# A Huber loss streamed through one core: half-row tiles in bf16 with POOL subtracting, against whole-row tiles in f32 worked in pieces by DVE and ACT

## The chip, the core and the metric

The kernel runs on one core of a Trainium2 chip. The metric is the device time of one execution in microseconds, the median of several runs. A core has compute engines with instruction queues of their own: VectorE (DVE), ScalarE (ACT), GpSimd (POOL) and TensorE (PE, unused here); SyncE (SP) issues transfers. The core's 16 DMA engines move data between HBM and the on-chip memory of 128 partitions. A transfer is issued by an instruction in the queue of SP, ACT or POOL and then runs by itself; semaphores tell when it has landed.

## The reference

```python
def reference(pred, target):            # both 8192 x 8192, float32
    delta = 1.0
    diff = pred - target
    abs_diff = np.abs(diff)
    return np.where(abs_diff <= delta, 0.5 * diff**2, delta * (abs_diff - 0.5 * delta))
```

Every element is read from two inputs and one result is written: 536.87 MB in, 268.44 MB out. Both kernels use the identity that with c the difference clamped to [-1, 1] (or min(|d|, 1)), the loss is c²/2 + max(|d| - 1, 0).

## The kernel before, in words

The 8192 rows are cut into 64 row tiles of 128 rows, one row on each partition, 8192 columns. A row tile's inputs come as two halves of 4096 columns, each a transfer of 2 MB per input (`emit_loads`, L46 to L58): `a` always from SP's queue, `b` from SP's for the first half and from ACT's for the second. The pools of `a` and `b` have three half-row buffers each (L37, L38), so one and a half row tiles of input fit.

For each row tile the loop (L92 to L115) first issues the loads of the next tile, then finishes the tile before (`do_tail`, L65: on ACT the square at L68 and the Relu of |d| - 1 at L69, on DVE the sum at L70), then has POOL subtract the halves and write the difference as bf16 (L103), then ACT takes the absolute value (L108) and DVE the minimum with 1 (L109). The result `sfull` is bf16; `flush` (L60) has POOL's queue issue its store, a transfer that casts bf16 to f32 on the way out (L63). So three compute engines share a tile, all on whole rows of 8192 columns in bf16 except for POOL's half rows.

What sets the order: each engine works through its queue as written. A load waits for a buffer, which POOL's subtraction at L103 frees. The subtraction waits for its two halves. The store at L63 stands in POOL's queue between subtractions.

The last two tiles (L117 to L226) are written out by hand in pieces of 2048 and 1024 columns. Some pieces go the way described, others on DVE alone (a clamp, a fused multiply-add and a product, as at L197, L200 and L203), and each piece has its own store from POOL's queue (L179, L191).

Of the kernel before, what the change touches and what calls it, by code (L numbers as in the profile page):

```python
# [6 lines left out]


@with_exitstack
def kernel(  # L10
# [6 lines left out]
    nc = tc.nc  # L17
    P = 128
    fp32 = mybir.dt.float32
    bf16 = mybir.dt.bfloat16  # L20
    Alu = mybir.AluOpType
    Act = mybir.ActivationFunctionType

    n_rows, n_cols = pred.shape
    COLS = 4096
    n_ct = n_cols // COLS
    SQRT_HALF = 0.70710678118654752
# [4 lines left out]
    n_rt = pred_t.shape[0]  # L32

    neg1 = nc.alloc_sbuf_tensor("huber_neg1_bf16", [P, 1], bf16)
    nc.gpsimd.memset(neg1.ap(), -1.0)
# [6 lines left out]
    loads = {}  # L42
    pending_tail = []
    pending_store = []

    def emit_loads(i):  # L46
        if i >= n_rt:
            return
        tl = []
        for j in range(n_ct):  # L50
            c0 = j * COLS
            a = pool_a.tile([P, COLS], fp32)
            b = pool_b.tile([P, COLS], fp32)
            nc.sync.dma_start(out=a, in_=pred_t[i, :, c0 : c0 + COLS])
            beng = nc.sync if j == 0 else nc.scalar
            beng.dma_start(out=b, in_=targ_t[i, :, c0 : c0 + COLS])
            tl.append((a, b))
        loads[i] = tl  # L58

    def flush(limit):  # L60
        while len(pending_store) > limit:
            r, pi = pending_store.pop(0)
            nc.gpsimd.dma_start(out=out_t[pi, :, :], in_=r)  # L63

    def do_tail(limit):  # L65
        while len(pending_tail) > limit:
            s, d, pi = pending_tail.pop(0)
            nc.scalar.activation(out=s, in_=s, func=Act.Square, scale=SQRT_HALF)  # L68
            nc.scalar.activation(out=d, in_=d, func=Act.Relu, bias=neg1.ap())  # L69
            nc.vector.tensor_tensor(out=s, in0=s, in1=d, op=Alu.add)  # L70
            pending_store.append((s, pi))

    def act_path(d, s):
        nc.scalar.activation(out=d, in_=d, func=Act.Abs)
        nc.vector.tensor_scalar(
            out=s, in0=d, scalar1=1.0, scalar2=None, op0=Alu.min
        )
        nc.scalar.activation(out=s, in_=s, func=Act.Square, scale=SQRT_HALF)
        nc.scalar.activation(out=d, in_=d, func=Act.Relu, bias=neg1.ap())
        nc.vector.tensor_tensor(out=s, in0=s, in1=d, op=Alu.add)  # L80

    def dve_path(d, s):
        nc.vector.tensor_scalar(
            out=s, in0=d, scalar1=-1.0, scalar2=1.0, op0=Alu.max, op1=Alu.min
        )
        nc.vector.scalar_tensor_tensor(
            out=d, in0=s, scalar=-0.5, in1=d, op0=Alu.mult, op1=Alu.add
        )
        nc.vector.tensor_tensor(out=s, in0=s, in1=d, op=Alu.mult)

    emit_loads(0)
    for i in range(n_rt - 2):  # L92
        dfull = pool_d.tile([P, n_cols], bf16)
        sfull = pool_s.tile([P, n_cols], bf16)

        emit_loads(i + 1)

        do_tail(0)

        for j in range(n_ct):  # L100
            c0 = j * COLS
            a, b = loads[i][j]
            nc.gpsimd.tensor_tensor(  # L103
                out=dfull[:, c0 : c0 + COLS], in0=a, in1=b, op=Alu.subtract
            )
        del loads[i]

        nc.scalar.activation(out=dfull, in_=dfull, func=Act.Abs)  # L108
        nc.vector.tensor_scalar(  # L109
            out=sfull, in0=dfull, scalar1=1.0, scalar2=None, op0=Alu.min,  # L110
        )

        flush(1)

        pending_tail.append((sfull, dfull, i))  # L115

    i62 = n_rt - 2  # L117
    i63 = n_rt - 1
    H = n_cols // 2

    d62 = pool_d.tile([P, n_cols], bf16, tag="dfull")
    s62 = pool_s.tile([P, n_cols], bf16, tag="sfull")

    emit_loads(i63)
    do_tail(0)

    for j in range(n_ct):
        c0 = j * COLS
        a, b = loads[i62][j]
        nc.gpsimd.tensor_tensor(  # L130
            out=d62[:, c0 : c0 + COLS], in0=a, in1=b, op=Alu.subtract
        )
    del loads[i62]

    flush(1)

    Q = 2048
    dq = [d62[:, k * Q : (k + 1) * Q] for k in range(4)]
    sq = [s62[:, k * Q : (k + 1) * Q] for k in range(4)]
    nc.scalar.activation(out=dq[0], in_=dq[0], func=Act.Abs)  # L140
    nc.vector.tensor_scalar(out=sq[0], in0=dq[0], scalar1=1.0, scalar2=None, op0=Alu.min)  # L141
    nc.vector.tensor_scalar(  # L142
        out=sq[1], in0=dq[1], scalar1=-1.0, scalar2=1.0, op0=Alu.max, op1=Alu.min
    )
# [45 lines left out]
    def st(lo, hi, s):  # L190
        nc.gpsimd.dma_start(out=out_t[i63, :, lo:hi], in_=s)  # L191
# [65 lines left out]
```

## Time and profile before

| | |
|---|---|
| median of the runs | 1923.07 us (4 runs, 1922.99 to 1923.16) |
| profiled execution | 1923.1 us, its span 1921.3 us |
| busy: DVE, ACT, POOL | 851.0, 1326.3, 1288.9 us |
| bytes moved by the DMA engines | 805.42 MB, mean 419 GB/s over the span |
| loads from SP's queue (q1) | 402.67 MB |
| loads from ACT's queue (q10) | 134.22 MB |
| stores from POOL's queue (q0) | 268.44 MB written |

The profile is of one execution. The span runs from its first to its last recorded instruction or transfer; the run's own time has 1.8 us more. A row of windows has the two ends of a stretch and its length, then for DVE, ACT and POOL the busy time and the number of instructions, the granted clock of TensorE, the mean busy share of the 16 DMA engines (packets that overlap can take it above 1) and the GB/s that they moved. Packets count with their ends, so windows of a few microseconds scatter. A row of groups has line, engine, operation, output and input, shapes and count, then the busy time in us and the mean of one in ns, then the idle time before and what ended it. In the timeline the columns are start, duration (over all merged instructions, waits between them included), engine, line and operation; SPq and ACTq are the queues' transfer-issuing instructions. In the list of DMA queues the columns after the name are packets, MB and the time that the packets took as a share of 16 engines' span.

### The profile page before, as it was taken

How to read it: one execution, taken by the hardware profiler on the slowest of the kernel's cores; microseconds unless marked ns; L12 is line 12 of the kernel's file. 1: busy time of each engine (PE TensorE's matmuls, PEld its weight loads, DVE VectorE, ACT ScalarE, POOL GpSimd, SP SyncE). 2: the span in 40 equal slices, each digit the busy share in tenths (PEclk: the TensorE clock that was granted, in tenths of full speed). 3: DMA queues.
4: the chain of work that ended last, by engine and by line, in shares of the span. 5: the costliest groups of instructions: out<-in, count | busy, mean ns of one | idle time of the engine just before them, and what ended most of it. 6: DMA issues, size and time to landing. Idle time of an engine off the chain costs nothing.

```text
span 1921.3 us, 1430 instructions
## 1 busy us (share of the span) xinstructions
DVE 851.0 (44%) x146; ACT 1326.3 (69%) x202; POOL 1288.9 (67%) x207
## 2 busy tenths in 40 slices
DVE  0344354453443534534435345344353443444566
ACT  2866767668677676686776866767768667676674
POOL 5686676766866767667677676676766866767664
DMA  9999999999999999999999999999999999999996
GB/s 405 377 422 423 423 427 423 426 424 425 425 423 426 426 424 426 420 426 425 426 422 427 425 425 425 424 424 425 427 424 425 424 423 425 425 425 424 425 429 271
DMA packets 47100, 805.42 MB, mean 419 GB/s; under 512 B 5233, under 2 KB 5233, under 8 KB 5489
## 3 DMA queue, kind: packets, MB, share of 16 engines
q1 hardware_dynamic: 27648, 402.67, 53.9%
q0 software_dynamic: 10224, 268.44, 32.9%
q10 hardware_dynamic: 9216, 134.22, 16.3%
q14 instruction: 12, 0.09, 0.0%
HBM read 536.87 MB, written 268.44 MB: 419 GB/s over the span
## 4 chain that ended last, share of the span: by engine, by line
ACT 51%; DVE 29%; issue 18%; DMA 1%; POOL 1%; ACTq 0%; POOLq 0%; SPq 0%
DVE sfull L109 28%; ACT dfull L108 23%; ACT sfull L68 22%; ACT dfull L69 5%; DMA b<-in_target_dram 1%; POOL dfull L103 1%; DVE s L153 1%; DVE s L142 0%; DVE sfull L70 0%; DVE s L194 0%; DVE d L147 0%; DVE d L159 0%; ACT d L158 0%; ACT s L195 0%; ACTq L252 0%
## 5 line engine op out<-in xcount | busy, mean ns | idle before, releaser
L103 POOL TENSOR_TENSOR dfull<-a,b 128x4096 bf16<-128x4096 f32 x124 | 1213.7, 9803 | 588.1 <-issue 559.0
L68 ACT ACTIVATE sfull<-sfull 128x8192 bf16<-128x8192 bf16 x62 | 435.9, 7030 | 532.8 <-DVE sfull L109 532.8
L70 DVE TENSOR_TENSOR sfull<-sfull,dfull 128x8192 bf16<-128x8192 bf16 x62 | 274.4, 4426 | 860.6 <-ACT dfull L69 860.6
L109 DVE TENSOR_SCALAR sfull<-dfull 128x8192 bf16<-128x8192 bf16 x62 | 528.7, 8527 | 194.8 <-ACT dfull L108 194.8
L108 ACT ACTIVATE dfull<-dfull 128x8192 bf16<-128x8192 bf16 x62 | 434.8, 7012 | 33.0 <-POOL dfull L103 33.0
L69 ACT ACTIVATE dfull<-dfull,huber_neg_bf 128x8192 bf16<-128x8192 bf16 x62 | 440.6, 7106 | 0.0
L63 POOL DMA_DIRECT2D out_dram<-sfull x62 | 35.7, 575 | 3.8 <-DVE sfull L70 3.8
L130 POOL TENSOR_TENSOR d<-a,b 128x4096 bf16<-128x4096 f32 x2 | 19.6, 9838 | 9.5 <-issue 9.5
L175 POOL TENSOR_TENSOR d<-a,b 128x2048 bf16<-128x2048 f32 (+1 forms) x5 | 18.1, 3643 | 0.1
L191 POOL DMA_DIRECT2D out_dram<-s x5 | 2.7, 540 | 11.7 <-DVE s L217 5.9
L153 DVE TENSOR_SCALAR s<-d 128x2048 bf16<-128x2048 bf16 x1 | 9.8, 9842 | 0.0
L142 DVE TENSOR_SCALAR s<-d 128x2048 bf16<-128x2048 bf16 x1 | 9.3, 9320 | 0.0
L179 POOL DMA_DIRECT2D out_dram<-s x4 | 2.2, 551 | 10.5 <-DVE s L152 4.2
L195 ACT ACTIVATE s<-s 128x2048 bf16<-128x2048 bf16 x1 | 1.9, 1911 | 8.1 <-DVE s L194 8.1
L162 DVE TENSOR_TENSOR s<-s,d 128x2048 bf16<-128x2048 bf16 x1 | 6.1, 6053 | 2.7 <-ACT d L158 2.7
L157 ACT ACTIVATE s<-s 128x2048 bf16<-128x2048 bf16 x1 | 1.9, 1910 | 6.0 <-DVE s L153 6.0
L145 ACT ACTIVATE s<-s 128x2048 bf16<-128x2048 bf16 x1 | 1.9, 1910 | 4.1 <-DVE s L141 4.1
L194 DVE TENSOR_SCALAR s<-d 128x2048 bf16<-128x2048 bf16 x1 | 3.3, 3276 | 0.0
L147 DVE SCALAR_TENSOR_TENSOR d<-s,d 128x2048 bf16<-128x2048 bf16 x1 | 2.3, 2293 | 0.0
L159 DVE SCALAR_TENSOR_TENSOR d<-s,d 128x2048 bf16<-128x2048 bf16 x1 | 2.3, 2283 | 0.0
L200 DVE SCALAR_TENSOR_TENSOR d<-s,d 128x2048 bf16<-128x2048 bf16 x1 | 2.3, 2278 | 0.0
L108 ACT ACT_TABLE_LOAD x1 | 1.3, 1283 | 1.2 <-PEq L241 1.2
(32 smaller groups left out, 34.7 us busy)
## 6 DMA issues: line engine op xcount, KB each, us to landing
a<-in_pred_dram SPq DMA_DIRECT2D x128, 2048.0 KB, 18.0
out_dram<-sfull POOLq DMA_DIRECT2D x62, 4096.0 KB, 20.1
b<-in_target_dram ACTq DMA_DIRECT2D x64, 2048.0 KB, 13.8
b<-in_target_dram SPq DMA_DIRECT2D x64, 2048.0 KB, 25.2
out_dram<-s POOLq DMA_DIRECT2D x7, 1024.0 KB, 4.9
out_dram<-s POOLq DMA_DIRECT2D x2, 512.0 KB, 5.0
```

What stands on the lines that cost most here:

```text
L63: nc.gpsimd.dma_start(out=out_t[pi, :, :], in_=r)
L68: nc.scalar.activation(out=s, in_=s, func=Act.Square, scale=SQRT_HALF)
L69: nc.scalar.activation(out=d, in_=d, func=Act.Relu, bias=neg1.ap())
L70: nc.vector.tensor_tensor(out=s, in0=s, in1=d, op=Alu.add)
L103: nc.gpsimd.tensor_tensor(out=dfull[:, c0 : c0 + COLS], in0=a, in1=b, op=Alu.subtract)
L108: nc.scalar.activation(out=dfull, in_=dfull, func=Act.Abs)
L109: nc.vector.tensor_scalar(out=sfull, in0=dfull, scalar1=1.0, scalar2=None, op0=Alu.min,)
L130: nc.gpsimd.tensor_tensor(out=d62[:, c0 : c0 + COLS], in0=a, in1=b, op=Alu.subtract)
L142: nc.vector.tensor_scalar(out=sq[1], in0=dq[1], scalar1=-1.0, scalar2=1.0, op0=Alu.max, op1=Alu.min)
L153: nc.vector.tensor_scalar(out=sq[2], in0=dq[2], scalar1=1.0, scalar2=None, op0=Alu.min)
L162: nc.vector.tensor_tensor(out=sq[2], in0=sq[2], in1=dq[2], op=Alu.add)
L175: nc.gpsimd.tensor_tensor(out=d63[:, lo:hi], in0=a[:, o0:o1], in1=b[:, o0:o1], op=Alu.subtract)
```

## The change

The kernel is written anew. It computes the same formula, in f32 throughout:

- A tile is a whole row tile, `a` and `b` in f32 of 8192 columns, three of each (`DEPTH`). A load is one transfer of 4 MB, all loads in SP's queue, `b` ahead of `a`. The loads of the last tile are split in four.
- Compute goes by pieces of 2048 columns, in place. `first` has DVE subtract (L58 of the new file) and clamp to [-1, 1] (L59), and ACT take Abs, Relu with bias -1 and the square (L62 to L64). `second` has DVE form 0.5 c² + max(|d| - 1, 0) (L69). `second` of a piece is written two pieces after its `first`, so it stands behind the first steps of the two following pieces in DVE's queue, of the next tile where need be.
- The stores copy f32 and are issued from ACT's queue, two of half a row for each tile (L53); the last tile has five.
- The loads of tile j + 3 are written after tile j's last `second`. `b` of it waits for that; `a` for the two stores of tile j.
- POOL is left with nothing in the loop. The order of SP, DVE and ACT is that of the code.

```diff
+P = 128
+ROW = 8192
+PIECE = 2048
+DEPTH = 3
...
-    pool_a = ctx.enter_context(tc.tile_pool(name="sbuf_a", bufs=3))
-    pool_b = ctx.enter_context(tc.tile_pool(name="sbuf_b", bufs=3))
-    pool_d = ctx.enter_context(tc.tile_pool(name="sbuf_d", bufs=2))
-    pool_s = ctx.enter_context(tc.tile_pool(name="sbuf_s", bufs=3))
+    pool_a = ctx.enter_context(tc.tile_pool(name="pool_a", bufs=DEPTH))
+    pool_b = ctx.enter_context(tc.tile_pool(name="pool_b", bufs=DEPTH))
...
+    def load(i, halves):
+        A[i] = pool_a.tile([P, ROW], f32, name="a")
+        B[i] = pool_b.tile([P, ROW], f32, name="b")
+        for lo, hi in halves:
+            nc.sync.dma_start(out=B[i][:, lo:hi], in_=targ_t[i, :, lo:hi])
+            nc.sync.dma_start(out=A[i][:, lo:hi], in_=pred_t[i, :, lo:hi])
...
-            nc.gpsimd.dma_start(out=out_t[pi, :, :], in_=r)
+    def store(i, lo, hi):
+        nc.scalar.dma_start(out=out_t[i, :, lo:hi], in_=A[i][:, lo:hi])
+
+    def first(i, lo, hi):
+        a, b = A[i][:, lo:hi], B[i][:, lo:hi]
+        nc.vector.tensor_tensor(out=a, in0=a, in1=b, op=Alu.subtract)
...
-            nc.gpsimd.tensor_tensor(
-                out=dfull[:, c0 : c0 + COLS], in0=a, in1=b, op=Alu.subtract
-            )
...
+            out=b, in0=a, scalar1=-1.0, scalar2=1.0, op0=Alu.max, op1=Alu.min
         )
+        nc.scalar.activation(out=a, in_=a, func=Act.Abs)
+        nc.scalar.activation(out=a, in_=a, func=Act.Relu, bias=neg1)
+        nc.scalar.activation(out=b, in_=b, func=Act.Square)
+    def second(i, lo, hi):
+        a, b = A[i][:, lo:hi], B[i][:, lo:hi]
         nc.vector.scalar_tensor_tensor(
+            out=a, in0=b, scalar=0.5, in1=a, op0=Alu.mult, op1=Alu.add
         )
...
+    with tc.manual_schedule(engines={Eng.SP, Eng.DVE, Eng.Activation}):
+        for i in range(DEPTH):
+            load(i, whole)
+        late = []
+        for i in range(n):
+            todo = pieces[:-1] + [(6144, 7168), (7168, ROW)] if i == n - 1 else pieces
+            for k, (lo, hi) in enumerate(todo):
+                first(i, lo, hi)
+                late.append((i, lo, hi))
+                if len(late) > 2:
+                    j, l, h = late.pop(0)
+                    second(j, l, h)
+                    if h == H and j < n - 1:
+                        store(j, 0, H)
+                    if h == ROW and j < n - 1:
+                        store(j, H, ROW)
+                        if j + DEPTH < n:
+                            load(j + DEPTH, split if j + DEPTH == n - 1 else whole)
+                    elif j == n - 1:
+                        store(j, l, h)
+        for j, l, h in late:
+            second(j, l, h)
+            store(j, l, h)
```

SP's queue at the start of the program, before: the loads of three half rows and then those that wait for a buffer. The names end in the number of the buffer's tile; brackets hold the semaphores that an instruction waits for (DMAHW: transfers, Pool: POOL's instructions).

```order
L54 DMA a_68<-in_pred_dram 128x4096
L56 DMA b_69<-in_target_dram 128x4096
L54 DMA a_72<-in_pred_dram 128x4096
L54 DMA a_78<-in_pred_dram 128x4096
L56 DMA b_79<-in_target_dram 128x4096
L54 DMA a_82<-in_pred_dram 128x4096 [waits DMAHW0_49,Pool_49]
L54 DMA a_92<-in_pred_dram 128x4096 [waits DMAHW3_49,Pool_49]
```

The same place in the changed kernel, with tiles 0, 1 and 2 and then tile 3 (`b_117`, `a_116`):

```order
L49 DMA b_69<-in_target_dram 128x8192
L50 DMA a_68<-in_pred_dram 128x8192
L49 DMA b_73<-in_target_dram 128x8192
L50 DMA a_72<-in_pred_dram 128x8192
L49 DMA b_77<-in_target_dram 128x8192
L50 DMA a_76<-in_pred_dram 128x8192
L49 DMA b_117<-in_target_dram 128x8192 [waits DMAHW0_49,DVE_49]
L50 DMA a_116<-in_pred_dram 128x8192 [waits DMAHW7_49,DMAHW5_49,DMAHW1_49]
```

Six whole loads stand ahead of the first that waits, and the wait for POOL has become one for DVE (`b`) and for two stores (`a`).

The store's place before, in POOL's queue between the subtractions of the third to fifth tile (`sfull_77` is the first tile's result):

```order
L103 TENSOR_TENSOR dfull_107<-a_92,b_93 128x4096 [waits DMAHW0_49,DMAHW1_49,DVE_49,Pool_49]
L103 TENSOR_TENSOR dfull_107<-a_96,b_97 128x4096 [waits DMAHW3_49,DMAHW2_49]
L63 DMA out_0_dram<-sfull_77 128x8192
L103 TENSOR_TENSOR dfull_125<-a_109,b_110 128x4096 [waits DMAHW4_49,DMAHW5_49,DVE_49,Pool_49]
L103 TENSOR_TENSOR dfull_125<-a_113,b_114 128x4096 [waits DMAHW7_49,DMAHW6_49]
```

And now, in ACT's queue (`a_68` is tile 0, `a_72` and `b_73` tile 1):

```order
L53 DMA out_0_dram<-a_68 128x4096 [waits DVE_49]
L62 ACTIVATE a_72<-a_72 128x2048 [waits DMAHW3_49,DVE_49]
L63 ACTIVATE a_72<-a_72,neg1_64 128x2048 [waits Activation_49]
L64 ACTIVATE b_73<-b_73 128x2048 [waits DMAHW2_49]
L62 ACTIVATE a_72<-a_72 128x2048 [waits DVE_49]
L63 ACTIVATE a_72<-a_72,neg1_64 128x2048 [waits Activation_49]
L64 ACTIVATE b_73<-b_73 128x2048
L53 DMA out_0_dram<-a_68 128x4096 [waits DVE_49]
L62 ACTIVATE a_72<-a_72 128x2048 [waits DVE_49]
```

The second half's store of tile 0 stands behind two pieces of tile 1, so behind tile 1's loads.

More of the change, by code (lines that the diff above doesn't have):

```diff
@@ L44 @@
[L44 to L58, printed above, removed]
@@ L92 @@
[L92 to L103, printed above, removed]
-                out=dfull[:, c0 : c0 + COLS], in0=a, in1=b, op=Alu.subtract
[L105 to L144, printed above, removed]
-    nc.scalar.activation(out=sq[0], in_=sq[0], func=Act.Square, scale=SQRT_HALF)
-    nc.scalar.activation(out=dq[0], in_=dq[0], func=Act.Relu, bias=neg1.ap())
-    nc.vector.scalar_tensor_tensor(
-        out=dq[1], in0=sq[1], scalar=-0.5, in1=dq[1], op0=Alu.mult, op1=Alu.add
-    )
```

120 lines of the change are left out of this document (13 added, 107 removed).

## Prediction

> **What bounds the kernel now.** I read the page first, then windows of the DMA rate, then the timeline of one row tile and the waits of SP. The page:
>
> ```profile
> span 1921.3 us, 1430 instructions
> ...
> DVE 851.0 (44%) x146; ACT 1326.3 (69%) x202; POOL 1288.9 (67%) x207
> ...
> GB/s 405 377 422 423 423 427 423 426 424 425 425 423 426 426 424 426 420 426 425 426 422 427 425 425 425 424 424 425 427 424 425 424 423 425 425 425 424 425 429 271
> ...
> q0 software_dynamic: 10224, 268.44, 32.9%
> q10 hardware_dynamic: 9216, 134.22, 16.3%
> ...
> HBM read 536.87 MB, written 268.44 MB: 419 GB/s over the span
> ```
>
> No compute engine is busy for more than 69%, while the data rate is flat from the second slice to the last but one. 536.87 + 268.44 = 805.31 MB must move in either kernel, so the time is this sum over the rate of the DMA engines, and what is lost at both ends. The windows tell whether that rate is all the engines can do:
>
> ```profile
> 5.00:35.00 30.00, 0.00 (x0) 0.00 (x0) 17.08 (x2) 1.00 1.01 430
> ...
> 96.00:1873.00 1777.00, 796.27 (x126) 1255.44 (x182) 1209.33 (x182) 1.00 1.05 425
> ...
> 623.60:649.20 25.60, 12.98 (x2) 16.93 (x3) 20.16 (x3) 1.00 1.06 431
> 653.20:678.90 25.70, 13.01 (x2) 17.03 (x3) 20.16 (x3) 1.00 1.06 429
> ...
> 620.20:623.40 3.20, 0.00 (x0) 3.20 (x1) 0.00 (x0) 1.00 1.05 394
> 649.80:653.00 3.20, 0.00 (x0) 3.20 (x1) 0.00 (x0) 1.00 1.05 420
> 679.50:682.70 3.20, 0.00 (x0) 3.20 (x2) 0.00 (x0) 1.00 0.95 358
> ...
> 798.00:801.20 3.20, 0.00 (x0) 3.20 (x1) 0.00 (x0) 1.00 1.02 384
> ```
>
> The last column is GB/s. With loads alone, all queued ahead (5 to 35 us), it is 430. In the steady part it is 425. But inside a row tile it is 429 to 431 for some 25.6 us, stores and loads mixed, and then dips to 358 to 420 for some 3 us (the windows are short against packets, so single ones scatter). So 430 is the rate that the engines give, with stores too, and the 425 is 430 with a hole in each tile. The timeline at the hole, and SP's largest wait:
>
> ```profile
> 598.49 19.64 POOL L103 TENSOR_TENSOR dfull<-a,b 128x4096 bf16<-128x4096 f32 x2 [9.47 <-issue]
> ...
> 607.32 11.17 SPq L54 DMA_DIRECT2D a<-in_pred_dram  x2
> 607.32 0.36 ACTq L56 DMA_DIRECT2D b<-in_target_dram  x1
> ...
> 618.07 0.57 POOL L63 DMA_DIRECT2D out_dram<-sfull  x1
> 618.57 0.90 SPq L56 DMA_DIRECT2D b<-in_target_dram  x1
> ```
>
> ```profile
> SPq L54 <- POOL dfull L103: 1710.9, 124, 17.7
> ```
>
> SP may issue a load only when POOL's subtraction gives a half-row buffer back. POOL ends its second subtraction at 618.1; only then come the next load, the other load and the store, all within 1.5 us. The earlier loads run out around 620, so the engines change over to transfers issued about 2 us before: that is the hole.
>
> **The change part by part.** *Where the 1921.3 us go now.* The ends and the ramp:
>
> ```profile
> 0.00:5.00 5.00, 0.00 (x0) 1.28 (x1) 0.30 (x5) 1.00 0.68 246
> 70.00:75.00 5.00, 5.00 (x1) 0.00 (x0) 5.00 (x2) 1.00 0.30 111
> ...
> 85.00:90.00 5.00, 0.00 (x0) 5.00 (x1) 0.38 (x1) 1.00 0.89 259
> ```
>
> ```profile
> 1890.00:1895.00 5.00, 5.00 (x1) 1.14 (x1) 4.33 (x2) 1.00 0.38 144
> 1895.00:1900.00 5.00, 5.00 (x4) 0.74 (x1) 2.92 (x2) 1.00 0.55 210
> 1900.00:1905.00 5.00, 3.98 (x4) 5.00 (x4) 0.96 (x2) 1.00 0.20 79
> 1905.00:1910.00 5.00, 3.79 (x6) 5.00 (x4) 0.15 (x1) 1.00 0.90 341
> 1910.00:1915.00 5.00, 1.45 (x2) 1.48 (x2) 1.59 (x3) 1.00 0.66 247
> 1915.00:1921.30 6.30, 0.00 (x0) 0.00 (x0) 0.00 (x0) 1.00 0.41 137
> ```
>
> A window loses its length times (1 - GB/s / 430). Start: 2.1 us. Ramp: 3.7 + 2.0 = 5.7. Tail: 3.3 + 2.6 + 4.1 + 1.0 + 2.1 + 4.3 = 17.4. The bytes at 430 take 1872.8. What is left of 1921.3 is 23.3 us, or 0.37 us for each of 62 tiles: the holes.
>
> *Holes and ramp.* The change puts three whole row tiles in flight (25.2 MB, 58.5 us of loading at 430), where before 1.5 were. Two questions decide whether the loads now stay ahead: does compute keep up, and is a buffer free in time?
>
> Compute. A tile may take 12.58 MB / 430 = 29.26 us, a 2048-column piece 7.3 us. The rows that price a piece:
>
> ```profile
> L200 DVE SCALAR_TENSOR_TENSOR d<-s,d 128x2048 bf16<-128x2048 bf16 x1 | 2.3, 2278 | 0.0
> ...
> L196 ACT ACTIVATE d<-d,huber_neg_bf 128x2048 bf16<-128x2048 bf16 x1 | 2.0, 1987 | 0.0
> ...
> L195 ACT ACTIVATE s<-s 128x2048 bf16<-128x2048 bf16 x1 | 1.9, 1911 | 8.1 <-DVE s L194 8.1
> ...
> L193 ACT ACTIVATE d<-d 128x2048 bf16<-128x2048 bf16 x1 | 1.9, 1893 | 0.0
> ...
> L197 DVE TENSOR_SCALAR s<-d 128x2048 bf16<-128x2048 bf16 x1 | 0.7, 681 | 0.0
> ```
>
> ACT does Abs, Relu and Square: 1.89 + 1.99 + 1.91 = 5.79 us a piece, if f32 costs what bf16 does (no f32 row is there). DVE does a subtraction and a fused multiply-add, which I take at the slowest row of this size, 2.28 each, and a clamp, which no row shows in f32: between 0.68 (bf16) and 2.28. That makes 5.2 to 6.8 us. All of it is under 7.3, so neither engine bounds, and the sum does not need the clamp's price. The Trainium skill ("VectorE: DVE Perf Modes", The perf-mode tier table) has an f32 tensor_scalar of this size at 1.23 us; by that DVE would take 5.8 us, an estimate that no row here shows.
>
> Buffers. A second half's store of tile j leaves only after the first two pieces of tile j+1 (the lag of two in `late`). Count from the landing of tile j+1's last load: subtraction and clamp 3.5 (2.28 and a clamp between its bounds), two pieces on ACT 11.6, the store's issue 0.4: it leaves at about 15.5. Its 2.1 MB take 4.9 us alone and up to 14.6 beside loads of twice the bytes; with some 2 us to land, A(j) is free at 23 to 32. B(j) is free at about 11. Queued from time 0 on are B and A of tile j+2 (19.5 us), B of tile j+3 (9.8) and the two half stores that leave at 15.5 and 27 (9.8): 39 us of work. The load that waited enters at 32 at the latest, 7 us before it is missed. So no hole: 23.3 us go. In the first turn tile 0's buffer comes back around 80 us, just as the queued loads end, with a store still running; I count the ramp's 5.7 as gone, with 3 us for the bound.
>
> The DMAs that move: stores go from POOL's queue, which cast bf16 to f32, to ACT's, which copies f32. q0 took 32.9% x 1921.3 x 16 / 268.44 = 37.7 engine-us per MB, q10 16.3% and 134.22 likewise 37.3, so I give the store no other price. ACT pays two issues of 0.36 a tile: 4 x 5.79 + 0.7 = 23.9 of 29.26 us. What is queued behind a store on ACT is the next piece; the store waits for DVE's multiply-add of a piece that is two behind, which is done by then, so it waits for nothing. Taking POOL out of the loop, and with it the bf16 tiles, costs and gives nothing by itself: it hid under the DMA.
>
> *Start.* Loads are issued as early as before: 2.1 us. That compute begins only after 8.4 MB (20 us) is hidden by the loads of tiles 1 and 2.
>
> *Tail.* The last store now and its landing, and ACT's half pieces:
>
> ```profile
> 1912.50 0.53 POOL L191 DMA_DIRECT2D out_dram<-s  x1 [0.40 <-DVE s L225]
> ```
>
> ```profile
> DMA to landing us min/median/max: 4.1/4.8/5.1
> ```
>
> ```profile
> L222 ACT ACTIVATE d<-d,huber_neg_bf 128x1024 bf16<-128x1024 bf16 x1 | 1.1, 1135 | 0.0
> L219 ACT ACTIVATE d<-d 128x1024 bf16<-128x1024 bf16 x1 | 1.0, 1042 | 0.0
> L221 ACT ACTIVATE s<-s 128x1024 bf16<-128x1024 bf16 x1 | 1.0, 1042 | 0.0
> ```
>
> 1912.5 + 4.8 = 1917.3; the span ends 4.0 later. I keep 3.8 of it as a fixed end. In the changed tail a piece's loads (2.1 MB) come every 4.9 us or, with stores between, 7.3; ACT needs 5.79, so it is about two pieces behind when the last load lands: 11.6 + two halves of 3.22 + issues 1.8 = 19.8, then the last multiply-add of 1024 columns (about 1.2, half of 2.28) and the store's landing 4.8: 26 us. In it the engines still move the last tile's 4.2 MB and two thirds of the 4.2 MB of the one before: 7.1 MB, 17 us. Lost: 9 (5 if ACT is one piece behind, 13 with the dear clamp).
>
> *Sum.* 1872.8 + 2.1 + 9 + 3.8 = 1887.7 of span; the profiled run took 1923.1 for a span of 1921.3, so 1.8 on top: **1889.5 us**. The profiled run is the median of the runs (1923.07), so nothing is to be corrected. Against 1923.1 that is 23.3 + 5.7 of holes and ramp, and 4.6 of tail.
>
> **The rivals.** *The rate stays at 425 (B).* For it: the number never leaves 423 to 427 for 1770 us, and a boundary between transfers may cost something however early they are issued. The Trainium skill ("DMA: Bandwidth & Descriptors", Issuing engines are not separate DMA queues) says that all queues run on the same 16 engines, so moving loads and stores between queues adds no bandwidth; the rows agree (430 with loads alone, 429 to 431 mixed). Against B: 5 to 35 us holds six transfers back to back without a dip. 805.31 / 425 = 1894.9, plus 16.7 for the rest: 1911.6 us.
>
> *The buffer comes too late (C), slower.* Place: SP's wait for A(j)'s second store. The margin is 7 us of 39. If the store lands later than 32 + 7 us (a dear clamp twice, f32 slower on ACT, a store starved by larger load packets), the engines go idle in each tile for the excess: 62 x 0.62 = 38 us reach 1927, so it decides from 7.6 us of delay on; at 9 us it gives about 1889.5 + 62 x 2 = 2013, at 8 us 1951. For it: three buffers, all held from load to store, and a store that waits on the next tile's load. Against it: the sum above uses the late ends already.
>
> *Stores from ACT's queue are dearer (D).* At 430 they take 624 us; 5% more is 31 us: 1920.7, no change. Against it: the rows of q0 and q10.
>
> **How the numbers follow.** Forecast 0.64 (1884 to 1904: the clamp's and tail's bounds, and a rate of 427 to 431), B 0.20, D 0.05, C 0.11. Less than 0.2% (3.8 us) can't be told from no change. Forecast and B are faster: 0.84. D is about 0.05 no change, C 0.11 slower. The range runs from 1884 (431 GB/s, tail loss 8) to 1912, which takes in B; outside lie C, D and a little below.
>
> **What would show it.** Right: a flat 429 to 431 GB/s in the middle slices; SP's waits long, but no dip at a tile's boundary; ACT near 1480 us (256 x 5.79) and DVE between 1340 and 1750 us; a last slice well over 271. Wrong: 425 in the middle (B), a dip of over 2 us in each 29 us (C), packets of q10 over 37.7 engine-us per MB (D), DVE over 1870 us.

## The result, and the profile after the change

The changed kernel takes 1879.26 us (median of 8 runs, 1877.24 to 1881.66) against 1923.09 us (median of 13 runs beside it): a ratio of 0.9773, with a 95% interval of 0.9763 to 0.9783. The forecast was 1889.5 us with a range from 1884 to 1912, so the time lies below the range: the direction was right, and the gain of 43.8 us is ten more than forecast. The profiled run took 1879.72 us for a span of 1877.9.

The page of the changed kernel, with the rows that answer to those shown of before (the q rows give packets, MB and the share of 16 engines' span):

```profile
span 1877.9 us, 2234 instructions
...
DVE 1446.8 (77%) x772; ACT 1447.8 (77%) x772; POOL 0.2 (0%) x4
...
GB/s 413 428 430 433 434 432 434 430 433 432 432 436 431 431 433 432 432 433 431 434 430 434 430 436 433 432 431 434 434 428 433 432 431 430 426 430 434 421 408 363
...
q1 hardware_dynamic: 19296, 536.88, 66.6%
q10 hardware_dynamic: 18864, 268.44, 33.4%
q14 instruction: 17, 0.14, 0.0%
```

The middle slices stand at 428 to 436 where they stood at 420 to 427, and the last slice at 363 instead of 271. What was not foreseen is at the right: 426, then 421 and 408 in the slices before the last. POOL is gone from the work. The stores' queue q10 took 33.4% x 1877.9 x 16 / 268.44 = 37.4 engine-us per MB, no more than POOL's queue (37.7) had.

The windows of the changed kernel (start and end, length, busy time of DVE, ACT and POOL, clock, DMA share, GB/s):

```profile
0.00:5.00 5.00, 0.06 (x1) 0.00 (x0) 0.20 (x4) 1.00 0.69 236
5.00:35.00 30.00, 12.07 (x7) 9.80 (x6) 0.00 (x0) 1.00 1.00 434
96.00:1500.00 1404.00, 1085.87 (x577) 1084.82 (x576) 0.00 (x0) 1.00 1.00 432
1500.00:1855.00 355.00, 279.58 (x150) 277.05 (x148) 0.00 (x0) 1.00 1.00 424
1855.00:1860.00 5.00, 4.97 (x3) 4.97 (x3) 0.00 (x0) 1.00 0.89 375
1860.00:1865.00 5.00, 4.97 (x5) 4.97 (x4) 0.00 (x0) 1.00 0.85 359
1865.00:1870.00 5.00, 4.97 (x4) 4.97 (x5) 0.00 (x0) 1.00 0.63 259
1870.00:1877.90 7.90, 3.02 (x3) 2.23 (x3) 0.00 (x0) 1.00 0.70 284
```

They give the ledger of the new span in the way in which the prediction made the old one, with 432.5 GB/s as the full rate (432 in the 1404 us of the middle, 433 in the half of it from 800 us on). The bytes take 805.31 / 432.5 = 1862.0 us. The start loses 5 x (1 - 236/432.5) = 2.3, the four windows from 1855 on lose 0.7 + 0.8 + 2.0 + 2.7 = 6.2, end included, the stretch from 1500 to 1855 loses 355 x (1 - 424/432.5) = 7.0, and 0.4 is left over, which fits a short dip near 50 us: 1877.9 in all.

The groups of the changed kernel, with shapes kept apart (count, busy us, mean ns of one, idle time before them):

```profile
L58 DVE TENSOR_TENSOR a<-a,b 128x2048 f32<-128x2048 f32 x255 | 582.8, 2285 | 416.5 <-DMA a<-in_pred_dram 224.4 <-issue 192.2
...
L59 DVE TENSOR_SCALAR b<-a 128x2048 f32<-128x2048 f32 x255 | 312.7, 1226 | 8.8
...
L62 ACT ACTIVATE a<-a 128x2048 f32<-128x2048 f32 x255 | 487.0, 1910 | 393.3 <-DVE b L59 393.3
...
L63 ACT ACTIVATE a<-a,neg 128x2048 f32<-128x2048 f32 x255 | 510.5, 2002 | 8.3
...
L64 ACT ACTIVATE b<-b 128x2048 f32<-128x2048 f32 x255 | 482.7, 1893 | 0.0
...
L69 DVE SCALAR_TENSOR_TENSOR a<-b,a 128x2048 f32<-128x2048 f32 x255 | 582.2, 2283 | 0.0
```

A piece costs ACT 1.91 + 2.00 + 1.89 = 5.80 us (5.79 forecast, so f32 costs ACT what bf16 did) and DVE 2.29 + 1.23 + 2.28 = 5.80. The clamp that no row showed takes 1.226 us, between the bounds of 0.68 and 2.28. The Trainium skill ("VectorE: DVE Perf Modes", The perf-mode tier table) had it at 1.23, and the trace agrees. Both engines are idle for 23% of the span: DVE ahead of its subtraction, where 224 us are put down to loads by name and 192 to "issue", and ACT while it waits for DVE.

### The profile page after: what moved, and what is told of

Its sections match the earlier page's. It is cut to its first block, busy times and chain, and to the rows that moved or that the text cites. A ratio compares the mean times of both kernels' runs of the same rounds, so it can differ in the third digit from the quotient of the medians.

```text
span 1877.9 us, 2234 instructions
## 1 busy us (share of the span) xinstructions
DVE 1446.8 (77%) x772; ACT 1447.8 (77%) x772; POOL 0.2 (0%) x4
## 3 DMA queue, kind: packets, MB, share of 16 engines
q10 hardware_dynamic: 18864, 268.44, 33.4%
HBM read 536.87 MB, written 268.44 MB: 429 GB/s over the span
## 4 chain that ended last, share of the span: by engine, by line
DMA 77%; ACT 13%; DVE 9%; issue 1%; another core or an unknown queue 0%; SPq 0%; DVEq 0%; ACTq 0%
DMA out_dram<-a 43%; DMA a<-in_pred_dram 34%; ACT a L62 6%; DVE a L58 5%; ACT a L63 4%; ACT b L64 3%; DVE b L59 3%; DVE a L69 1%; DVEq L58 0%; SPq L50 0%; SPq L49 0%; ACTq L53 0%
## 5 line engine op out<-in xcount | busy, mean ns | idle before, releaser
L58 DVE TENSOR_TENSOR a<-a,b 128x2048 f32<-128x2048 f32 (+1 forms) x257 | 585.2, 2277 | 416.5 <-DMA a<-in_pred_dram 224.4
L62 ACT ACTIVATE a<-a 128x2048 f32<-128x2048 f32 (+1 forms) x257 | 489.1, 1903 | 393.3 <-DVE b L59 393.3
L69 DVE SCALAR_TENSOR_TENSOR a<-b,a 128x2048 f32<-128x2048 f32 (+1 forms) x257 | 584.6, 2275 | 0.5 <-ACT b L64 0.5
L63 ACT ACTIVATE a<-a,neg 128x2048 f32<-128x2048 f32 (+1 forms) x257 | 512.8, 1995 | 8.3
L64 ACT ACTIVATE b<-b 128x2048 f32<-128x2048 f32 (+1 forms) x257 | 484.8, 1886 | 0.0
L59 DVE TENSOR_SCALAR b<-a 128x2048 f32<-128x2048 f32 (+1 forms) x257 | 314.1, 1222 | 8.9
```

Source lines behind the costliest of these rows:

```text
L58: nc.vector.tensor_tensor(out=a, in0=a, in1=b, op=Alu.subtract)
L59: nc.vector.tensor_scalar(out=b, in0=a, scalar1=-1.0, scalar2=1.0, op0=Alu.max, op1=Alu.min)
L62: nc.scalar.activation(out=a, in_=a, func=Act.Abs)
L63: nc.scalar.activation(out=a, in_=a, func=Act.Relu, bias=neg1)
L64: nc.scalar.activation(out=b, in_=b, func=Act.Square)
L69: nc.vector.scalar_tensor_tensor(out=a, in0=b, scalar=0.5, in1=a, op0=Alu.mult, op1=Alu.add)
```

## The experiments

The forecast missed on the side of too little gain, so two questions were open: whether the old kernel's holes had the cause that the prediction gave (loads issued too late, because SP waited for POOL to give a buffer back), and where the ten extra microseconds came from. All ratios below are against the kernel before.

**e1: the kernel before with one more buffer for each operand.** If loads are late because buffers come back late, a fourth buffer lets them be issued half a tile sooner. To fit it in, the `s` tiles lose 32 columns, and the last 32 columns of each row's result are not computed or stored (1.05 MB, 2.4 us of transfers).

```diff
-    pool_a = ctx.enter_context(tc.tile_pool(name="sbuf_a", bufs=3))
-    pool_b = ctx.enter_context(tc.tile_pool(name="sbuf_b", bufs=3))
+    pool_a = ctx.enter_context(tc.tile_pool(name="sbuf_a", bufs=4))
+    pool_b = ctx.enter_context(tc.tile_pool(name="sbuf_b", bufs=4))
```

> The kernel before with four half-row buffers of each input in place of three, so that loads are issued half a row tile (15 us) earlier. To make room the last 32 columns of each row's result are left out, 1.05 MB or 2.4 us of stores. Theory: the dip to 358-420 GB/s in each tile comes from loads issued about 2 us before the engines need them, and it goes: 62 x 0.37 = 23 us, with the 2.4 us 1897.7 us, and up to 6 us less if the ramp's stall goes too. Rival (the lower rate comes from the casting stores of POOL's queue or from half-row loads, not from late loads): the dips stay and the time is 1920.7 us.

Measured: 1918.55 us, ratio 0.9975 (0.9966 to 0.9985): 4.6 us less, of which 2.4 are the bytes left out. The windows of e1:

```profile
96.00:300.00 204.00, 89.39 (x14) 143.46 (x22) 139.88 (x21) 1.00 1.02 431
300.00:600.00 300.00, 131.82 (x22) 213.12 (x31) 204.29 (x31) 1.00 1.06 426
600.00:1800.00 1200.00, 527.81 (x81) 845.86 (x122) 823.61 (x123) 1.00 1.08 425
```

The extra lead holds the rate at 431 only until it is used up, some 300 us into the span; then 425 is back for good. So something other than the loads' lead holds each tile to the time that 425 GB/s would take, and the prediction's account of the holes falls.

*A second account of the kernel before.* POOL's first subtractions stand 29.63 us apart there, in every tile from the third on to within 0.01 us, and 12.58 MB / 29.63 us = 425 GB/s. So the period might be set by compute, with the transfers only following. The chain that ended last, on the page of the kernel before, which the prediction had not weighed:

```profile
ACT 51%; DVE 29%; issue 18%; DMA 1%; POOL 1%; ACTq 0%; POOLq 0%; SPq 0%
```

DMA holds 1% of it. (POOL has 1% too: the chain counts a minimum that is held up as DVE's own work.) The timeline of the kernel before, from the minimum of one tile to that of the next (POOL's subtraction of the first stands in the prediction, at 598.49):

```profile
600.83 8.60 DVE L109 TENSOR_SCALAR sfull<-dfull 128x8192 bf16<-128x8192 bf16 x1 [2.49 <-ACT dfull L108]
...
609.47 7.03 ACT L68 ACTIVATE sfull<-sfull 128x8192 bf16<-128x8192 bf16 x1 [8.67 <-DVE sfull L109]
616.41 7.11 ACT L69 ACTIVATE dfull<-dfull,huber_neg_bf 128x8192 bf16<-128x8192 bf16 x1
...
623.55 4.43 DVE L70 TENSOR_TENSOR sfull<-sfull,dfull 128x8192 bf16<-128x8192 bf16 x1 [14.11 <-ACT dfull L69]
628.12 8.80 POOL L103 TENSOR_TENSOR dfull<-a,b 128x4096 bf16<-128x4096 f32 x1 [9.48 <-issue]
630.47 8.60 DVE L109 TENSOR_SCALAR sfull<-dfull 128x8192 bf16<-128x8192 bf16 x1 [2.50 <-ACT dfull L108]
```

These steps close a ring. DVE's sum L70 ends at 627.98 and POOL's first half starts at 628.12: `dfull` has two buffers, and the sum is the last to read the one that POOL writes next (the profile calls this wait "issue"). That half takes 8.80 us. The minimum L109 starts beside it, but ends only 2.14 us after it (639.07; POOL's half ends at 636.92). Square, Relu and the sum follow. 8.80 + 2.14 + 6.98 + 7.11 + 4.46 + 0.14 between them make the period of 29.63 us.

The link that stands out is the minimum: 8.6 us, of which only the last 2.1 come after POOL's half. POOL's two halves together took 19.64 us (the row at 598.49), so its second half took 10.84, two more than the first. It looks as if each held up the other in turn. The Trainium skill ("SBUF — State Buffer", Who interferes with whom) says that DVE in its two-port modes shares a pair of ports with GpSimd, and that whoever issues first holds it for a whole instruction while the other stands still; these rows agree. If the minimum were not held, it would end at 603.2 and the ring would take some 23 us (an estimate from these rows), less than the 29.3 of the transfers. By this account the loads come late because POOL waits for the ring, and the dips of the rate are its shadow. Two experiments on the kernel before change the ring and leave buffers, loads and bytes as they are.

**e5: the kernel before with Abs and the minimum in two halves.** The first half of the minimum can then run before POOL starts.

```diff
-        nc.scalar.activation(out=dfull, in_=dfull, func=Act.Abs)
-        nc.vector.tensor_scalar(
-            out=sfull, in0=dfull, scalar1=1.0, scalar2=None, op0=Alu.min,
-        )
+        for j in range(n_ct):
+            h = slice(j * COLS, (j + 1) * COLS)
+            nc.scalar.activation(out=dfull[:, h], in_=dfull[:, h], func=Act.Abs)
+            nc.vector.tensor_scalar(
+                out=sfull[:, h], in0=dfull[:, h], scalar1=1.0, scalar2=None, op0=Alu.min,
+            )
```

> The kernel before with the absolute value (ACT) and the minimum (DVE) of each tile cut into two halves of 4096 columns; same buffers, same transfers. In the trace before, a tile's period is the sum of four instructions that wait for each other: Abs 7.0, minimum 8.6, Square 7.0, Relu 7.1 = 29.6 us. New theory: this ring sets the period, and the dips in the DMA rate are only its shadow; with halves the minimum's first half runs beside the second half of Abs, the ring falls to some 22 to 26 us, the DMA engines become the bound at 430 GB/s, and the time falls by 20 to 26 us, to 1897 to 1903 us. Rival (the prediction's: loads are issued too late for want of buffers): the buffers are as before, the dips stay, 1920 to 1924 us.

Measured: 1906.32 us, ratio 0.9912 (0.9896 to 0.9929), 17 us less. The timeline of e5, at the start of POOL's work on a tile:

```profile
619.70 1.22 DVE L111 TENSOR_SCALAR sfull<-dfull 128x4096 bf16<-128x4096 bf16 x1
619.87 9.71 POOL L103 TENSOR_TENSOR dfull<-a,b 128x4096 bf16<-128x4096 f32 x1 [9.41 <-DVE sfull L70]
622.37 8.29 DVE L111 TENSOR_SCALAR sfull<-dfull 128x4096 bf16<-128x4096 bf16 x1 [1.45 <-ACT dfull L110]
```

POOL's wait is put down to DVE's sum L70 by name here: the link that was "issue" before. The same half minimum takes 1.22 us ahead of POOL and 8.29 beside it, so its length is POOL's and not its own. And the halving gains next to nothing: the second half ends 1.08 us after POOL's subtraction instead of 2.14, but the first half holds up that subtraction in its turn (9.71 us instead of 8.80). 10.79 stand where 10.94 stood, and POOL's period falls only from 29.63 to 29.42 us. That times 62 tiles is 13 of the 17 us. The expectation had summed the ring in another way, as Abs, minimum, Square and Relu, which makes 29.6 us too; by that sum the halving should have brought 22 to 26 us. It did not, and the sum through POOL's half gives what was measured.

**e9: the kernel before with a pause inside POOL's first half.** The first subtraction is cut into two of 2048 columns, and POOL's store issue stands between them instead of behind both halves. No buffer, queue or transfer is added; the cut and the store's place change together.

```diff
-        for j in range(n_ct):
-            c0 = j * COLS
-            a, b = loads[i][j]
+        for c0, w in ((0, 2048), (2048, 2048), (4096, 4096)):
+            a, b = loads[i][c0 // COLS]
+            o = c0 % COLS
             nc.gpsimd.tensor_tensor(
-                out=dfull[:, c0 : c0 + COLS], in0=a, in1=b, op=Alu.subtract
+                out=dfull[:, c0 : c0 + w], in0=a[:, o : o + w], in1=b[:, o : o + w],
+                op=Alu.subtract,
             )
+            if c0 == 0:
+                flush(1)
...
-        flush(1)
```

> The kernel before with POOL's first subtraction of a tile (4096 columns, 9.8 us) cut into two of 2048 and the store's issue moved between them, so that POOL leaves off for a moment after 4.9 us. The halved minimum of the run before still ended 1 us after POOL's first subtraction. Theory: DVE's minimum is held up while that subtraction runs, so a tile's ring is DVE sum 4.4, POOL's first subtraction 9.8, the rest of the minimum 1.1, Square 7.0, Relu 7.1 = 29.4 to 29.6 us; with the shorter subtraction it is about 25, the DMA engines become the bound and the time is 1895 to 1904 us. Rival (the minimum takes 8.6 us by itself and the ring is Abs, minimum, Square, Relu): no change, 1920 to 1924 us.

Measured: 1891.62 us, ratio 0.9835 (0.9822 to 0.9849): 31.6 us less, over two thirds of what the whole change brings. From e9's groups, its waits, the chain on its page, and its windows:

```profile
L112 DVE TENSOR_SCALAR sfull<-dfull 128x8192 bf16<-128x8192 bf16 x62 | 149.9, 2418 | 212.6 <-ACT dfull L111 212.6
```

```profile
POOL dfull L103 <- DMA b<-in_target_dram: 642.0, 59, 17.1
```

```profile
DMA 63%; POOL 27%; issue 6%; DVE 2%; ACT 1%; SPq 1%; ACTq 0%; POOLq 0%
```

```profile
70.00:75.00 5.00, 2.07 (x1) 2.90 (x1) 4.98 (x2) 1.00 0.75 318
...
96.00:1840.00 1744.00, 589.56 (x126) 1263.32 (x181) 1098.75 (x240) 1.00 1.04 431
```

With the minimum let in after 4.5 us of POOL instead of 8.8 the ring should take 4.3 us less, 25.3. The timeline of e9 shows it at that length in the first tiles, before POOL has to wait for data:

```profile
65.41 4.50 POOL L103 TENSOR_TENSOR dfull<-a,b 128x2048 bf16<-128x2048 f32 x1 [8.42 <-DVE sfull L70]
67.77 4.29 DVE L112 TENSOR_SCALAR sfull<-dfull 128x8192 bf16<-128x8192 bf16 x1 [2.49 <-ACT dfull L111]
...
90.73 4.50 POOL L103 TENSOR_TENSOR dfull<-a,b 128x2048 bf16<-128x2048 f32 x1 [5.22 <-issue]
```

The two subtractions stand 25.32 us apart, and so does the next one. Afterwards the ring no longer decides: POOL waits for data, the minimum finds POOL idle and takes 2.4 us instead of 8.5, and DMA has 63% of the chain that had 1% of it. (Now and then it is DVE's sum that POOL holds up, off the path.) The steady rate is 431 with the same buffers, queues and transfers as before: the holes were the ring's. The ramp shrinks with them (318 GB/s from 70 to 75 us, where 111 stood), so most of it was the ring as well. Which of the two edits, the cut or the store's place, does how much of this was not taken apart. The store's place is not in the sum of the ring, so the cut is the likelier.

**e2: the changed kernel with half-row loads.** Each operand of a tile comes in two transfers of 16 KB rows, as before the change, instead of one of 32 KB rows.

```diff
-    whole = [(0, ROW)]
+    whole = [(0, H), (H, ROW)]
```

> The changed kernel with each whole-row load cut into two half-row loads (packets of 16 KB instead of 32 KB), nothing else. Theory: the rate above the forecast (431 to 434 GB/s against 430) comes from the larger load packets, so it falls back to 430 and the time rises by 8 to 11 us, to 1887 to 1890 us. Rival (the rate rose because the casting stores are gone): no change, 1877 to 1882 us.

Measured: 1885.13 us, ratio 0.9802 (0.9787 to 0.9816), 5.9 us more than the changed kernel. The steady window of e2:

```profile
96.00:1800.00 1704.00, 1320.12 (x698) 1319.31 (x699) 0.00 (x0) 1.00 1.01 431
```

It holds 430.7 GB/s where the changed kernel holds 432.5, or 7.8 us over all bytes. In the packet records a 16 KB load packet takes 611 ns and a 32 KB one 1213, 26.8 and 27.0 bytes a ns. So the longer rows are worth some 6 to 8 us, less than the 8 to 11 expected, and 431 is the rate of the old rows when nothing holds them back, in e2 as in e9.

**e3: the changed kernel with a lag of one piece.** The second half's store leaves a piece sooner, so the load that waits for it does too (rival C).

```diff
-                if len(late) > 2:
+                if len(late) > 1:
```

> The changed kernel with the second step written one piece after the first instead of two, so each store leaves one piece (5.7 us) earlier and its buffer comes back that much sooner. The trace of the changed kernel has three of the 16 DMA engines 7 to 11 us behind the others at 1500 us, and from there on dips to 402-424 GB/s. Theory (the slowest DMA engine sets the time, the others only wait for it): the other engines may run ahead further and the dips may go, but the time stays within 2 us of 1879. Rival (the buffer comes back too late, as the prediction's case C has it): the dips go and the time falls by 5 to 7 us, to 1872 to 1874 us.

Measured: 1881.38 us, ratio 0.9782 (0.9767 to 0.9797), 2 us more than the changed kernel. A late window, first of the changed kernel and then of e3:

```profile
1500.00:1820.00 320.00, 247.59 (x132) 248.60 (x132) 0.00 (x0) 1.00 1.00 428
...
1500.00:1820.00 320.00, 250.69 (x132) 249.53 (x132) 0.00 (x0) 1.00 1.00 432
```

The sooner store removes the dips there, worth 3 us (320 x 4/432.5), and the time does not fall: in the windows from 1820 us to the end e3 loses 13.9 us against the full rate, the changed kernel 9.3. So the dips are where the buffer comes late (C does bite, late in the program). The timelines show where the gain goes. In the changed kernel the last whole load (`a` of the last tile but one) lands at 1822.7 us. From there on DVE goes from one instruction to the next without a wait for a load, and the last store lands 54.4 us later. In e3 that load lands 1.5 us sooner, but 57.3 us follow it: with a lag of one, DVE waits for ACT's square three times in the last two tiles (1.97, 1.51 and 2.12 us).

**What lags.** The trace's records show when each of the 16 DMA engines finished its part of a store, without the engine's number. This is how far the last one ended behind the first in the changed kernel, at seven stores:

```
us in the span    192   585   715   975  1236  1498  1630
us of spread      2.8   3.1   4.9   7.2   9.2  10.1  11.5
```

At the last two of them thirteen engines are within 0.7 us of each other; three are behind, by 6.9, 8.7 and 11.5 us at the last one. The lag grows in steps.

Steps of one engine, 0.4 to 1.2 us each, follow within 21 us a packet of the queue of instructions (q14: 17 packets of 8 KB). The packet records show the delay itself: the 8 load packets between 96 and 1500 us that took over 0.1 us more than the usual 1.213 us all stand beside such a packet, and took 0.25 to 0.57 us more. About half of the lag comes in another kind of step, of all three at once (at 676, 968, 1114 and 1231 us), whose cause is open.

A store has landed only when its slowest engine is done, and a load of `a` waits for two stores, so the lag eats the 7 us by which the prediction's waiting load was early; from some 1520 us on it is gone, and the rate dips. The next run multiplies what is suspected.

**e4: the changed kernel with 6000 tiny instructions on idle POOL.** They add instruction packets, and nothing waits for them.

```diff
+    scratch = const.tile([P, 1], f32)
+    for _ in range(6000):
+        nc.gpsimd.memset(scratch[0:1, :], 0.0)
```

> The changed kernel with 6000 one-element memsets on POOL at its start, which nothing waits for; the result is the same. POOL otherwise idles. Each 8 KB packet of the instruction queue (17 in the changed kernel) seems to be followed by a step of about 1.2 us in the spread of the 16 engines' landings. Theory: fetching instructions delays the DMA engine that does it; some 47 more packets appear and the slowest engine loses up to 47 x 1.2 = 56 us if they all fall on it, some 10 to 30 us if on several. Rival (the steps are chance): more packets but no change, 1877 to 1882 us.

Measured: 1906.61 us, ratio 0.9915 (0.9900 to 0.9930), 27.4 us more than the changed kernel. From e4's page and windows:

```profile
q14 instruction: 64, 0.52, 0.1%
```

```profile
96.00:500.00 404.00, 302.09 (x161) 299.41 (x160) 265.69 (x2399) 1.00 1.00 423
500.00:1000.00 500.00, 376.06 (x200) 379.51 (x202) 329.14 (x2963) 1.00 1.00 417
1100.00:1800.00 700.00, 544.02 (x290) 543.94 (x290) 0.00 (x0) 1.00 1.01 432
```

While POOL runs through its instructions the rate is 417 to 423, and afterwards 432. DVE and ACT are as busy as without them (1447 us each). 47 more packets go with 27.4 us more, 0.58 us each, and the stores' spread alternates between 9 and 14 us from some 200 us on. With the delayed load packets above, this shows that the fetching of instructions costs transfer time; that the instructions themselves, of one element each, cost nothing is argued. A packet itself takes 0.31 us on its engine; why it costs more than that stays open.

**e6: the changed kernel in pieces of 4096 columns** (lag of one piece, the last tile in small pieces as before): half the instructions.

```diff
-PIECE = 2048
+PIECE = 4096
...
-            todo = pieces[:-1] + [(6144, 7168), (7168, ROW)] if i == n - 1 else pieces
+            todo = split[:-1] + [(6144, 7168), (7168, ROW)] if i == n - 1 else pieces
...
-                if len(late) > 2:
+                if len(late) > 1:
```

> The changed kernel with pieces of 4096 columns (lag one piece, so the same columns of lag), the last tile in pieces as it was: about half the compute instructions. Theory (each fetch of an instruction packet costs its DMA engine about 0.6 to 1.2 us, and the slowest engine sets the time): about half the fetches, the slowest engine loses about half of its 11 us, 1873 to 1876 us, if the longer pieces don't starve a buffer. Rival (fetches are harmless in this number): 1878 to 1882 us.

Measured: 1879.03 us (1878.97 to 1879.10), ratio 0.9770 (0.9756 to 0.9785): the changed kernel's time, as the rival had it. Its page and a window:

```profile
q14 instruction: 11, 0.09, 0.0%
```

```profile
1500.00:1820.00 320.00, 241.62 (x67) 238.30 (x66) 0.00 (x0) 1.00 1.00 432
```

There are no late dips, and the last load lands at 1855.8 us, 5.6 us sooner than in the changed kernel (1861.4). The gain goes again at the end: with big pieces in the tile before the last, compute is further behind when the last load lands, and 20.7 us follow it until the last store has landed, instead of 15.7.

**e10: e6 with the last two tiles in pieces of 2048 columns** and the lag of two there, so that both gains can be had.

```diff
-            todo = split[:-1] + [(6144, 7168), (7168, ROW)] if i == n - 1 else pieces
+            todo = pieces if i < n - 2 else split
+            if i == n - 1:
+                todo = split[:-1] + [(6144, 7168), (7168, ROW)]
...
-                if len(late) > 1:
+                if len(late) > (1 if i < n - 2 else 2):
```

> The changed kernel with pieces of 4096 columns for the first 62 tiles (lag one piece) and of 2048 for the last two (lag two). With big pieces throughout, the last load landed 5.6 us sooner and the tail behind it was 4.9 us longer. Theory: fewer instruction fetches leave the slowest engine less behind, and small pieces at the end bring the tail back to 16 to 18 us: 1873 to 1876 us, faster than both kernels. Rival (the tail is longer because the loads end sooner, whatever the pieces): 1878 to 1880 us.

Measured: 1874.19 us (1873.93 to 1874.60), ratio 0.9745 (0.9732 to 0.9759): 5.1 us under the changed kernel, and the two intervals do not meet. The last whole load lands at 1817.0 us, 5.7 us sooner than in the changed kernel, and 54.4 us follow it until the last store has landed, as many as there. This version beats both kernels. How much of the 5.7 us is due to fewer instruction packets is not shown: the larger pieces change more than that, and e3 and e7 land this load 1.5 and 2.1 us sooner with 17 and 18 packets.

**e7: the changed kernel with its stores in POOL's queue** (rival D from the other side).

```diff
-        nc.scalar.dma_start(out=out_t[i, :, lo:hi], in_=A[i][:, lo:hi])
+        nc.gpsimd.dma_start(out=out_t[i, :, lo:hi], in_=A[i][:, lo:hi])
```

> The changed kernel with its stores issued from POOL's queue (f32 to f32) instead of ACT's. It tells what the queue is worth. Theory: the rate in the middle stays at 430 to 433 GB/s, and the program's end gets back the 3 us that a kernel with transfers in POOL's queue took from its last landing to the end of the span (3.8 against 0.9 us), and the stores land about 1 us later: 1881 to 1886 us. Rival (the queue of POOL itself is slower, for want of descriptors while DVE clamps): the rate falls to 425 or below and the time is 1905 us or more.

Measured: 1879.48 us, ratio 0.9773 (0.9758 to 0.9787): the same as the changed kernel, and under the 1881 to 1886 expected. The queue of e7's page took 33.4% x 1877.6 x 16 / 268.44 = 37.4 engine-us per MB, just as ACT's:

```profile
q0 software_dynamic: 18864, 268.44, 33.4%
```

So the queue moves bytes neither faster nor slower, which agrees with the Trainium skill ("DMA: Bandwidth & Descriptors", Issuing engines are not separate DMA queues). After the last landing the program's end is 1.0 us longer, where 3 were expected. What made up for it was not foreseen: e7 has no dips from 1500 to 1820 us (432 GB/s), its stores' spread stays at 7.2 us or less, and its last whole load lands 2.1 us sooner. Why the spread is smaller is open.

**e8: the changed kernel with two buffers instead of three** (one run), to see rival C's price where it must decide.

```diff
-DEPTH = 3
+DEPTH = 2
```

> The changed kernel with two whole-row buffers of each input instead of three: the price of case C. By the walk in the prediction a buffer comes back 23 to 32 us after the next tile's loads have landed and then has to be loaded, 10 to 14 us: a period of 35 to 40 us instead of 29.1, 2250 to 2600 us. Rival (the buffers have far more slack than the walk says): below 2000 us.

Measured: 2779.38 us, more than the 2250 to 2600 expected. The timeline of e8 over one tile:

```profile
699.01 2.29 DVE L58 TENSOR_TENSOR a<-a,b 128x2048 f32<-128x2048 f32 x1 [21.40 <-DMA a<-in_pred_dram]
...
721.79 0.34 ACTq L53 DMA_DIRECT2D out_dram<-a  x1
728.10 0.33 SPq L50 DMA_DIRECT2D a<-in_pred_dram  x1
```

The next tile's first subtraction stands at 742.68, so a tile takes 43.7 us. The load that waits for the store is issued 6.3 us after it, and DVE stands still for some 21 us in all until its data are there. C's mechanism is real; the third buffer is what keeps it off the path.

## Why the prediction was wrong, and where it was right

Two terms of its sum were mis-sized, the rate by 10.8 us and the tail and end by 6.6, and they put the time below its range. The largest part of the gain, the holes and the ramp, came out in size, but for another cause than the one given.

*Holes and ramp: the size right, the cause wrong.* The step "then the engines change over to transfers issued about 2 us before: that is the hole" took what follows for the cause. The loads were late since POOL was late, POOL waited for the ring, and the ring was closed by a minimum that POOL itself held up. A fourth buffer gave 2 us beyond its bytes (e1); letting the minimum in sooner gave 31.6 (e9). The 23.3 and 5.7 us were priced from the windows and not from the cause. The change happens to take POOL out altogether, so both still go; that is luck, since what the prediction relied on, loads issued sooner, gives 2 us where it was tried alone. The prediction read the row `598.49 ... POOL L103 ... [9.47 <-issue]` and went on to SP's waits; the page's chain, with 51% ACT, 29% DVE and 1% DMA, said that transfers did not end last.

*"Taking POOL out of the loop ... costs and gives nothing by itself": wrong by the same cause.* Taking it out is what opens the ring.

*Rate: mis-sized by 10.8 us, the largest miss.* 430 GB/s was called "the rate that the engines give". It is what 16 KB rows show in short windows; over the long windows of e2 and e9 they give 431, and the changed kernel's 32 KB rows give 432.5. 1872.8 became 1862.0. The packets' size, which the diff shows, was given no term; e2 puts 6 to 8 us on it. Rival B (425) falls: the number was the ring's period and not a cost of changing transfers.

*Tail and end: 6.6 us too much.* 9 + 3.8 were forecast, 6.2 measured. From the timeline of the changed kernel's end:

```profile
1822.80 2.29 DVE L58 TENSOR_TENSOR a<-a,b 128x2048 f32<-128x2048 f32 x1 [7.23 <-DMA a<-in_pred_dram]
...
1860.36 1.91 ACT L62 ACTIVATE a<-a 128x2048 f32<-128x2048 f32 x1
...
1872.29 1.23 DVE L69 SCALAR_TENSOR_TENSOR a<-b,a 128x1024 f32<-128x1024 f32 x1 [0.50 <-ACT b L64]
```

The last load landed at 1861.4 us, when ACT had just started on the last whole piece: it was one piece behind and not two, the case that the prediction priced at 5. The last store has landed 3.6 us after the last multiply-add (4.8 forecast), at 1877.1, and the span ends 0.8 us later. The 3.8 us taken as a fixed end belonged to the old kernel (3.7 after its last landing); with POOL issuing the stores (e7) it is 1.8. The first row shows what the prediction's walk over the tail did not look at: it is DVE's last wait for a load, and for the 54 us behind it the pace is that of DVE and ACT (4.97 us busy of each 5 in the windows from 1855 to 1870).

*A term that was missing: the late dips, 7 us the other way.* Of these, 3 us fall before 1820 us, where a sooner store (e3) removes them; by the account above they are what the engines' lag costs. The rest falls between 1820 and 1855 us, where e3 loses 2.8 us and e7 4.3, and its cause was not tested. No row of the kernel before showed the lag: its stores' spread goes up and down between 0.6 and 4.2 us and does not grow, probably because the dips in each tile let the slow engines catch up. That the fetching of instructions costs transfer time is shown by e4 and the packets beside it; that it is the whole of the lag is not shown.

*Together* against the forecast span of 1887.7: rate -10.8, tail and end -6.6, start +0.2, late dips +7.0, the early dip +0.4, which makes 1877.9.

*Compute and buffers: right.* ACT's three rows sum to 1480 us (1480 forecast; with overlapping ends counted once, the page has 1448), DVE's to 1478, inside 1340 to 1750. SP's waits in the changed kernel are long and harmless until late:

```profile
SPq L50 <- DMA out_dram<-a: 1611.9, 91, 27.2
...
SPq L49 <- DVE a L69: 153.6, 61, 40.6
```

C's margin of 7 us was used up by the lag, as far as the times of the two tell; giving it back (e3) did not help, since the lag of one made the end longer by more. D fell with e7.

The changed kernel's own runs scatter by 4.4 us, while those of the kernel before, e6 and e7 stay within 0.4; where the instruction packets fall in a run would be one explanation, which was not tested.

## What to carry to other kernels

Before a dip in the transfers is put down to late loads, read the chain that ended last. If DMA is hardly in it, divide a tile's bytes by the dip-ridden rate and look for steps that release one another in turn and add up to that period: such a ring of compute and buffers sets the pace, and one more load buffer will buy next to nothing. That an instruction recurs at the period is not enough, as every engine has its share of each tile; here it recurred to within 0.01 us, and in e9, where transfers decide, every other period is 28.6 us and the next 29.9. An instruction that takes several times as long beside another engine as alone (8.29 against 1.22 us here) is the link to look at first. Once transfers are the bound, the length of their rows, the number of instructions to be fetched and what compute still has to do when the last whole load lands are worth a few microseconds each.

## What the runs showed of the hardware

- Beside POOL's subtractions DVE's bf16 minimum ends only some 2 us after POOL's instruction, be that 8.80 us long (before) or 4.50 (e9), and POOL's next one is longer by about as much: 8.5 us against 2.4 for the minimum, 10.84 against 8.80 for POOL's half.
- A load packet beside an instruction packet took 0.25 to 0.57 us more than its 1.213 in the changed kernel. Single DMA engines fall behind after such packets and do not catch up while all are busy: up to 11.5 us of spread at 1630 us, 27.4 us of time with 47 more packets (e4).
- One core alone sustained 432.5 GB/s of mixed loads and stores over 1400 us with 32 KB rows, and 430.7 with 16 KB rows.
- The time from the last landing to the end of the span is 0.8 us in the changed kernel, 1.8 with POOL's queue for the stores and 3.7 before.
